# A bias table built beside another attention, and an S5 matrix read from its rows by distance

## The chip, the cores and the metric

The kernel runs on one core of one Trainium2 chip. The metric is the device time of the whole program in microseconds, the median of several runs. A core has TensorE (PE in the profile; PEld is its weight load), VectorE (DVE), ScalarE (ACT), GpSimd (POOL) and SyncE (SP). Here SP issues nearly all DMAs, and it issues them in the order of its queue: an issue that must wait for a buffer holds back all that stand behind it. The kernel before takes 1791.37 us in the median of 3 runs (1785.62 to 1793.07).

## The reference, cut to what matters

The model has two layers over 512 latent and 256 context tokens, width 1024. Each layer sends the modulated input through one wide projection (`h @ w_in`) and then through three mixers: (A) an S5 state-space layer with a gate, (B) neighbourhood attention on the latent grid with a learned relative-position bias, (C) latent attention with compressed keys and values. The branches are gated, projected, added, and projected once more, with a residual and a layer norm.

The change touches two tables that depend on parameters alone, not on tokens:

```python
# (B) the bias: a table looked up by row and column distance, plus a column mask
bias  = rpb[:, idx_r, idx_c].reshape(H, rows, GRID_W, n_lat)
s_lat = einsum('brqhd,brkhd->bhrqk', qr, kg) * NA_SCALE + bias
s_lat = where(mask, s_lat, NEG_INF)
# (A) the scan over time, s_t = a * s_(t-1) + B u_t,  y_t = C s_t, both directions
```

The kernel works (A) out in chunks of 8 tokens. Within a chunk the outputs are the inputs times a block-Toeplitz matrix: its 16 x 16 blocks depend only on the distance j - j', of which there are 15.

## The kernel before, in words

Every matmul of weights with activations is done three times with split operands (high x high, low x high, high x low), in `gemm` at line 232. A weight block arrives by DMA in one of 4 buffers `wr` (`wraw`, line 215), is split by ACT (`wh`) and by DVE or POOL (`wl`), and is then used.

A layer goes through five phases, each with its own SBUF pools:

1. `s5a`: the projections for S5, the gates of branches, the compressed columns (`compressed`, line 1051) and the S5 matrices. `s5_build` makes, for each of 4 blocks of 8 groups, the input, output and scan matrices and the table of 15 distances `kds` (line 683 stores it to DRAM as `kd`, named `s_k` in the profile). Layer 0 builds its four blocks here; layer 1 builds its last two here.
2. `na`: four rounds, each with one `s5_block` (the scan of one block) and the neighbourhood attention of two heads. Line 753 loads the matrix of the chunk, `tp`, into one of 2 buffers `s5_w`; line 758 multiplies it with the inputs.
3. `mla`: four rounds of latent attention for two heads. Behind each round stand gate projections (`gate_n`, `gate_s`) whose result lies in one of 2 buffers `g_t` until it has been stored.
4. `mrg`: the three branch projections, the merge gates, the GELU and gate of S5. `mod_step` works on the next layer's modulation, and in layer 0 `SIDE` puts work for layer 1 between the steps: letter by letter, `T` the S5 tables, `B` one S5 build, `N` the attention bias, `G` the GELU. The GELU's pool takes the place of the pools of T and B, so it waits until these are done with.
5. `outp`: the output projection, the residual and the norm.

Two places matter here. First, at the end of each build, eight DMAs from DRAM to DRAM (line 686) write the matrix of the chunk out in full, `td` (`s_t` in the profile), 16 of its 128 rows each; line 753 later reads it in one piece. Secondly, `na_bias_layer` (lines 350 to 364) makes the bias of one layer: for each head (or two) three DMAs fetch shifted rows of the padded table `rpb_d` into a tile (line 361), POOL adds the column mask `na_mk` (line 145 of the helper), and one DMA stores it to `na_zd` (line 363). Layer 0's bias is made in `s5a`; layer 1's at `N` in `mrg`, in tiles `sb` of the build's ring of 4. The rounds of `na` read `na_zd` at line 1162.

The order of instructions on each engine and on SP is not written by hand: a planner goes through the program with its own estimate of times, and on each engine takes the ready instruction that comes first in the program.

Of the kernel before, what the change touches and what calls it, by code (L numbers as in the profile page):

```python
# [77 lines left out]
SB = (6, 4, 6)  # L78
# [3 lines left out]
SE = {'out0': (2, (1,)), 'out1': (2, (1,)), 'mla0': (4, (0,)), 'mla1': (2, (1,)), 's5a1': (1, (0,)), 'mrg0': (1, (0,)), 'na0': (1, (0,)), 'na1': (1, (0,))}  # L82
SE_REST = (3, (0,))

SIDE = ('T....B.B..N...G.........', '................G.......')

GX = ((0, 0, 1, 1), (1, 1, 1, 0))

# [31 lines left out]
def build(tc, a, out):  # L120
    nc = tc.nc
    V, S, P, PE = nc.vector, nc.scalar, nc.gpsimd, nc.tensor
    Q, PQ = nc.sync, nc.gpsimd
# [7 lines left out]
    def T(p, shape, tag, bufs=1, dt=F32):  # L131
        if isinstance(p, dict):
            p = p.get(tag, p[None])
        return p.tile(list(shape), dt, name=tag, tag=tag, bufs=bufs)
# [22 lines left out]
    dr = pool("dr", DRAM)  # L157
# [45 lines left out]
    def split(h, l, f):  # L203

        act(h, f)
        flip[0] += 1
        n, dve = SE0 if where[0] == "s5a0" else SE.get(where[0], SE_REST)
        e = V if flip[0] % n in dve else P
        tt(e, l, f, h.bitcast(F32), ALU.subtract)
# [140 lines left out]
    def na_bias_layer(l, pd, p, tag, bufs, size):  # L350

        mk = T(p, [48, 32], "na_mk")
        Q.dma_start(out=mk, in_=a["k_namask"])
        zd = T(dr, [48, 8, 480], f"na_zd{l}")
        nh = size // 480
        for h in range(0, 8, nh):
            z = T(p, [128, size + size // 5], tag, bufs)[0:48, 0:480 * nh].rearrange("p (r c) -> p r c", c=32)
            for ty in range(3):
                src = bass.AP(tensor=pd.tensor, offset=pd.offset + (l * 8 + h) * 960 + 8 * ty,
                              ap=[[1, 16], [64, 15 * nh], [1, 32]])  # L360
                Q.dma_start(out=z[16 * ty:16 * ty + 16], in_=src)
            tt(P, z, z, mk.unsqueeze(1).to_broadcast([48, 15 * nh, 32]), ALU.add)
            Q.dma_start(out=zd[:, h:h + nh], in_=z.rearrange("p (h r) c -> p h (r c)", h=nh))
        return zd


    def s5_loads(l, wk, q_=Q):
# [193 lines left out]
    def s5_build(l, b, prm, wk, ng, nsb, ni, out_q=Q):  # L561
# [14 lines left out]
        wd = [T(dr, [128, 1024], f"s5_w{l}{b}{d}") for d in range(2)]  # L576
        od = [T(dr, [128, 1152], f"s5_o{l}{b}{d}") for d in range(2)]
        rd = [T(dr, [128, 2, 384], f"s5_r{l}{b}{d}") for d in range(2)]
        td = T(dr, [128, 8, 128], f"s5_t{l}{b}")
        kd = T(dr, [2, 128, 240], f"s5_k{l}{b}")  # L580
        dcol = dcols[:, l, b]
        gs = slice(8 * b, 8 * b + 8)
# [98 lines left out]
                act(w[:, 128 * g0:128 * (g0 + ng)], q[:, 0:128 * ng])  # L681
            out_q.dma_start(out=wd[d], in_=w)
        out_q.dma_start(out=kd.rearrange("x q n -> q x n"), in_=kds.rearrange("p x m i -> p x (m i)"))
        for j in range(8):
            src = bass.AP(tensor=kd.tensor, offset=kd.offset + (7 - j) * 16, ap=[[240, 16], [32 * 240, 8], [1, 128]])
            Q.dma_start(out=td[16 * j:16 * j + 16], in_=src)
        mats[l].append((wd, od, td, rd))


    def s5_block(mats, b, m8, ud, yd, p, need_ctx):  # L690
        NY = 96 if need_ctx else 64
        wd, od, td, rd = mats
        u = T(p, [128, 8, 128], "s5_u", 1)
        uv = ud.rearrange("(g i) j c -> j i g c", i=16)
        for j in range(8):
            Q.dma_start(out=u[16 * j:16 * j + 16], in_=uv[j])
        sd = [T(p, [128, 8, 128], "s5_s0"), T(p, [128, 8, 97], "s5_s1")]
        P.memset(sd[0][:, :, 0], 0.0)
        P.memset(sd[1][:, :, 96], 0.0)
        ot = []  # L700
        for d in range(2):
            k0 = d * 16 + 4 * b
            w = T(p, [128, 8, 128], "s5_w", 2)
            Q.dma_start(out=w.rearrange("p g n -> p (g n)"), in_=wd[d])
            rc = T(p, [128, 2, 4, 96], "s5_rc", 1)
            Q.dma_start(out=rc.rearrange("p z c n -> p z (c n)"), in_=rd[d])
            o = T(p, [128, 1136], "s5_o", 2)
            Q.dma_start(out=o, in_=od[d][:, 16:1152] if d == 0 else od[d][:, 0:1136])
            ot.append([o[:, 144 * g:144 * g + 128] for g in range(8)])

            mg = T(p, [128, 4, 96], "s5_mg", 1)
            act(mg, m8[:, k0:k0 + 4].unsqueeze(2).to_broadcast([128, 4, 96]))
            P.memset(mg[:, :, 0 if d == 0 else 95], 0.0)

            pv = psw().rearrange("p (r x) -> p r x", r=2)[:, :, 0:384].rearrange("p r (e c) -> p r e c", e=4)
            for r in range(2):
                for g in range(8):
                    e = g % 2
                    PE.matmul(pv[64 * e:64 * e + 64, r, g // 2], w[:, g, 64 * r:64 * r + 64],  # L719
                              u[:, g, 32 * d:32 * d + 96], start=True, stop=True)  # L720

            cv, sv = rc[:, 0], rc[:, 1]
            if d == 1:
                cv, sv = cv[:, :, ::-1], sv[:, :, ::-1]
            va = T(p, [128, 2, 4, 96], "s5_va")
            vb = T(p, [128, 2, 4, 96], "s5_vb")
            for r in range(2):
                tt(V, va[:, r], pv[:, r], cv, ALU.mult)
                tt(V, vb[:, r], pv[:, r], sv, ALU.mult)
            vp = T(p, [128, 2, 384], "s5_vp")  # L730
            fl = lambda z: z.rearrange("p e c -> p (e c)")
            tt(V, vp[:, 0], fl(va[:, 0]), fl(vb[:, 1]), ALU.add)
            tt(V, vp[:, 1], fl(va[:, 1]), fl(vb[:, 0]), ALU.subtract)
            for r in range(2):
                x, m_ = vp[:, r], fl(mg)
                if d == 1:
                    x, m_ = x[:, ::-1], m_[:, ::-1]
                V.tensor_tensor_scan(out=x, data0=m_, data1=x, initial=0.0, op0=ALU.mult, op1=ALU.add)
            va = T(p, [128, 2, 4, 96], "s5_va")
            vb = T(p, [128, 2, 4, 96], "s5_vb")  # L740
            vpv = vp.rearrange("p r (e c) -> p r e c", e=4)
            for r in range(2):
                tt(V, va[:, r], vpv[:, r], cv, ALU.mult)
                tt(V, vb[:, r], vpv[:, r], sv, ALU.mult)
            c_ = slice(1, 97) if d == 0 else slice(0, 96)
            for e in range(2):
                q = slice(64 * e, 64 * e + 64)
                tt(V, sd[d][0:64, e::2, c_], va[q, 0], vb[q, 1], ALU.subtract)
                tt(V, sd[d][64:128, e::2, c_], va[q, 1], vb[q, 0], ALU.add)
        if need_ctx:  # L750
            V.tensor_copy(out=sd[0][:, :, 96:128], in_=sd[0][:, :, 0:32])
        tp = T(p, [128, 8, 128], "s5_w", 2)
        Q.dma_start(out=tp, in_=td)
        ys = T(p, [128, 2, 4, 96], "s5_va").rearrange("p a b c -> p (a b) c")
        py = psw()
        for g in range(8):
            o = py[:, 512 * (g // 4) + 96 * (g % 4):][:, 0:NY]
            PE.matmul(o, tp[:, g], u[:, g, 32:32 + NY], start=True, stop=False)  # L758
            PE.matmul(o, ot[0][g], sd[0][:, g, 32:32 + NY], start=False, stop=False)
            PE.matmul(o, ot[1][g], sd[1][:, g, 1:1 + NY], start=False, stop=True)  # L760
        for s in range(2):
            act(ys[:, 4 * s:4 * s + 4, 0:NY],
                py[:, 512 * s:512 * s + 384].rearrange("p (g c) -> p g c", g=4)[:, :, 0:NY])
        yv = yd.rearrange("(g i) j c -> j i g c", i=16)
        for j in range(8):
            Q.dma_start(out=yv[j][:, :, 0:NY], in_=ys[16 * j:16 * j + 16, :, 0:NY])
# [60 lines left out]
    with st:  # L827
# [5 lines left out]
        mats = [[], []]  # L833
# [4 lines left out]
        for l in range(DEPTH):  # L838
# [40 lines left out]
            with phase("s5a", 3, 2, 1, 1) as sa:  # L879
# [141 lines left out]

                def biases(_):
                    pds.append(na_bias_rows(sp))
                    zds.append(na_bias_layer(0, pds[0], sa, "sb", SB[0], 960))

# [236 lines left out]
            with phase("mla", 2, 2, 2, groups=G_MLA) as mp:  # L1264
# [8 lines left out]
                def gate_n(m):  # L1273
                    th = gate(mp, C_GN + 128 * m)
                    Q.dma_start(out=gn_d[m][:, 0:n_tok], in_=th[:, 0:n_tok])
# [34 lines left out]
                for k in range(2):  # L1310
                    f = early((128, n_tok), c_d[k][:, 0:n_tok])
                    split(cqh[:, k, 0:n_tok], cql[:, k, 0:n_tok], f)

                v_t = T(mp, [128, 6, 512], "mla_v")
                for t in range(6):
# [5 lines left out]
                for i in range(4):  # L1321
# [89 lines left out]
                    Q.dma_start(out=a_m[i][:, 0:n_tok], in_=am[:, 0:n_tok])  # L1411
                    if i < 3:
                        gate_n(2 * i + 2)
                        gate_n(2 * i + 3)
                    for _ in range(GX[l][i]):
                        gate_s(len(ga))

# [2 lines left out]
            with phase("mrg", 4, 3, 0, 1, groups=G_MRG) as mg, contextlib.ExitStack() as es:  # L1420
# [34 lines left out]
                def next_build():  # L1455
                    s5_build(l + 1, len(mats[l + 1]), side["prm"], side["b"], 4, SB[1], NI[1])

                def next_bias():
                    zds.append(na_bias_layer(l + 1, pds[0], side["b"], "sb", SB[1], 480))

                def gelu():

                    sides.close()
# [25 lines left out]
                def side_step(m):  # L1489
                    j = SIDE[l][m]  # L1490
                    if j == "G":
                        gelu()
                    elif j in "TBN" and need_ctx:
                        {"T": next_tables, "B": next_build, "N": next_bias}[j]()

                get = branch_w("w_branch_b")
                for m in range(8):
# [169 lines left out]
```

## Time and profile before

| | |
|---|---|
| median of 3 runs | 1791.37 us (1785.62 to 1793.07) |
| the profiled execution | 1788.85 us, its span 1787.1 us |
| PE busy | 1655.7 us, 93% of the span |
| PEld / DVE / ACT / POOL busy | 78% / 69% / 42% / 21% |
| mean granted TensorE clock | 0.973 of full speed |
| DMA | 264.87 MB, the 16 engines busy for 49.4% with the hardware queue |

The span begins with the first and ends with the last instruction; the profiled execution's own time is 1.75 us longer. The phases of layer 0 lie at about 0 to 225 us (`s5a`), 225 to 490 (`na`), 490 to 702 (`mla`), 702 to 962 (`mrg`) and 962 to 1085 (`outp`); those of layer 1 at 1085 to 1205, 1205 to 1420, 1420 to 1580, 1580 to 1705 and 1705 to the end. In a row of the timeline the first number is the start, the second the duration (with x8, of the eight together), and what stands in brackets is the idle time of that engine just before, with what ended it.

### The profile page before, as it was taken

The page shows a single profiled execution, that of the slowest core. Times are in us where ns is not written, and L with a number is a line of the kernel's source. Part 1 is how long each engine was busy: PE and PEld are TensorE (multiplying, and loading weights), DVE is VectorE, ACT ScalarE, POOL GpSimd, SP SyncE. Part 2 cuts the span into 40 slices and gives each one's busy share as a digit, 9 for nine tenths or more (in the row PEclk, how much of TensorE's full clock was granted, in tenths as well). Part 3 has the DMA queues.
Part 4 walks back from the last instruction along what each step waited for, and adds up shares of the span by engine and source line. Part 5 has one row for each costly group of instructions (what it writes and reads, how often), then busy time and mean ns, then how long its engine had stood idle before and what let it go on. Part 6 is the DMA issues. An engine that isn't in the chain of part 4 may idle for free.

```text
span 1787.1 us, 29011 instructions
## 1 busy us (share of the span) xinstructions
PE 1655.7 (93%) x10808; PEld 1387.4 (78%) x10808; DVE 1238.3 (69%) x2722; ACT 746.9 (42%) x1466; POOL 379.7 (21%) x284
## 2 busy tenths in 40 slices
PE   4899699999989999999799988899999999999996
PEld 2687588888878888878688767788888888788865
DVE  4899948877746564989357688838888666762257
ACT  4423344335355565222243345442344555642241
POOL 2000111012221101201403542001111311245382
PEclk9899799999999999999899999999999999999999
DMA  9567785345321122655756726755554422253462
GB/s 307 158 191 222 207 248 153 94 143 141 84 78 56 58 69 97 232 164 170 192 167 219 189 90 192 225 162 164 156 165 120 126 76 65 83 154 106 130 206 71
DMA packets 273076, 264.87 MB, mean 148 GB/s; under 512 B 70440, under 2 KB 227896, under 8 KB 272936
## 3 DMA queue, kind: packets, MB, share of 16 engines
q1 hardware_dynamic: 271736, 259.93, 49.4%
q0 software_dynamic: 1200, 3.10, 0.5%
q8 instruction: 85, 1.39, 0.3%
q14 instruction: 55, 0.45, 0.1%
HBM read 198.64 MB, written 68.53 MB: 149 GB/s over the span
## 4 chain that ended last, share of the span: by engine, by line
PE 59%; DVE 13%; DMA 6%; ACT 3%; issue 2%; POOL 2%; SPq 1%; DVEq 0%; ACTq 0%; POOLq 0%
PE g L232 35%; PE s L197 5%; PE w L1375 4%; PE s L1403 3%; PE g L1608 2%; DVE sb L145 2%; PE w L1174 2%; PE s L1213 2%; PE w L719 1%; DVE wl L145 1%; DVE ln_rs L148 1%; DMA y<-y_d 1%; DMA wr<-in_w_out 1%; POOL macc L145 1%; PE w L758 1%
## 5 line engine op out<-in xcount | busy, mean ns | idle before, releaser
L232 PE MATMUL g<-hh,wh 128*128 128x512 f32 (+1 forms) x1344 | 479.3, 358 | 16.3 <-ACT wh L142 11.9
L232 PE MATMUL g<-hl,wh 128*128 128x512 f32 (+1 forms) x1344 | 477.0, 355 | 2.7 <-POOL hl L145 1.5
L232 PE MATMUL g<-hh,wl 128*128 128x512 f32 (+1 forms) x1344 | 475.9, 355 | 1.1 <-DVE wl L145 1.1
L232 PEld LDWEIGHTS g<-hh,wh 128*128 128x128 f32 x1344 | 256.3, 191 | 55.9 <-ACT wh L142 12.8
L232 PEld LDWEIGHTS g<-hl,wh 128*128 128x128 f32 x1344 | 256.4, 191 | 37.7 <-DVE hl L148 2.5
L232 PEld LDWEIGHTS g<-hh,wl 128*128 128x128 f32 x1344 | 255.9, 190 | 36.9 <-DVE wl L145 2.8
L142 ACT ACTIVATE wh<-wr 128x1024 fp32r<-128x1024 f32 (+1 forms) x150 | 155.2, 1036 | 227.4 <-PE g L232 139.8
L145 DVE TENSOR_TENSOR wl<-wr,wh 128x1024 fp32r<-128x1024 f32 (+1 forms) x118 | 153.6, 1305 | 114.0 <-ACT wh L142 113.3
L232 PE MATMUL g<-al,wh 128*128 128x512 f32 (+1 forms) x336 | 120.4, 359 | 1.8 <-DVE al L145 1.8
L232 PE MATMUL g<-ah,wl 128*128 128x512 f32 (+1 forms) x336 | 118.7, 358 | 1.2 <-POOL wl L145 1.1
L232 PE MATMUL g<-ah,wh 128*128 128x512 f32 (+1 forms) x336 | 119.7, 361 | 0.0
L145 POOL TENSOR_TENSOR wl<-wr,wh 128x1024 fp32r<-128x1024 f32 (+1 forms) x32 | 74.9, 2339 | 201.7 <-ACT wh L142 183.9
L142 ACT ACTIVATE mla_pt<-s 128x384 f32<-128x384 f32 (+1 forms) x128 | 59.4, 475 | 86.5 <-PE s L197 85.9
L1377 DVE TENSOR_REDUCE mla_sm<-w 128x1 f32<-128x768 f32 (+1 forms) x80 | 67.9, 849 | 34.2 <-PE w L1375 33.3
L145 POOL TENSOR_TENSOR macc<-macc,g_t 128x768 f32<-128x768 f32 (+1 forms) x32 | 56.5, 1769 | 146.3 <-DVE g_t L148 146.3
L232 PEld LDWEIGHTS g<-ah,wh 128*128 128x128 f32 x336 | 63.4, 189 | 14.4 <-issue 3.1
L142 ACT ACTIVATE na_p<-w,na_sm 128x512 f32<-128x512 f32 (+1 forms) x80 | 50.8, 643 | 54.6 <-DVE na_sm L152 48.3
L232 PEld LDWEIGHTS g<-al,wh 128*128 128x128 f32 x336 | 63.9, 190 | 12.3 <-DVE al L145 2.5
L232 PEld LDWEIGHTS g<-ah,wl 128*128 128x128 f32 x336 | 63.9, 190 | 11.6 <-POOL wl L145 2.5
L1608 PE MATMUL g<-woh,hh 128*128 128x512 f32 (+1 forms) x168 | 64.9, 386 | 4.3 <-ACT woh L142 4.2
L142 ACT ACTIVATE mla_p<-w,mla_sm 128x768 f32<-128x768 f32 (+1 forms) x80 | 65.0, 813 | 4.7 <-DVE mla_sm L152 4.5
L1608 PE MATMUL g<-woh,hl 128*128 128x512 f32 (+1 forms) x168 | 64.5, 384 | 0.0
(350 smaller groups left out, 3417.5 us busy)
## 6 DMA issues: line engine op xcount, KB each, us to landing
wr<-in_w_in SPq DMA_DIRECT2D x104, 512.0 KB, 4.6
wr<-in_w_mod SPq DMA_DIRECT2D x32, 512.0 KB, 4.6
s_w<-s_w SPq DMA_DIRECT2D x32, 512.0 KB, 4.3
s_o<-s_o SPq DMA_DIRECT2D x16, 568.0 KB, 5.8
wr<-in_w_out SPq DMA_DIRECT2D x16, 512.0 KB, 3.6
s_o<-sb SPq DMA_DIRECT2D x12, 576.0 KB, 4.4
wr<-in_w_in SPq DMA_DIRECT2D x16, 416.0 KB, 4.6
s_rc<-s_r SPq DMA_DIRECT2D x16, 384.0 KB, 3.2
```

The lines of the kernel that those rows point to most:

```text
L142: return S.activation(out=o, in_=i, func=f, **kw)
L145: return e.tensor_tensor(out=o, in0=x, in1=y, op=op)
L148: V.scalar_tensor_tensor(out=o, in0=x, scalar=s, in1=y, op0=op0, op1=op1)
L197: PE.transpose(o, i, ident[:n, :n])
L232: PE.matmul(o, w[:, k], x[:, k, 0:n], start=(k == 0 and i == 0), stop=(k == nk - 1 and i == 2))
L719: PE.matmul(pv[64 * e:64 * e + 64, r, g // 2], w[:, g, 64 * r:64 * r + 64], u[:, g, 32 * d:32 * d + 96], start=True, stop=True)
L1174: PE.matmul(q[:, e, c:c + 256], qs[:, e, cq], k_[:, e, w0:w0 + 256], start=(j == 0), stop=(j == 1))
L1213: PE.matmul(po[64 * e:64 * e + 64, 0:128], v_t[:, t, 64 * e:64 * e + 64], pt[:, e, n], start=(n == 0), stop=(n == len(kt) - 1))
L1375: PE.matmul(q[:, c], x[0:96, cq], y[0:96, c], start=(j == 0), stop=(j == 2))
L1377: V.tensor_reduce(out=sm[:, 3:4], in_=q[:, k0:TOK], axis=AX.X, op=ALU.max)
L1403: PE.matmul(po[64 * e_:64 * e_ + 64, 0:128], v_t[:, t, 128 * i + 64 * e_:128 * i + 64 * e_ + 64], p2[e_][:, n], start=(n == 0), stop=(n == ...
L1608: PE.matmul(o, x[:, k, tok], w[k][:, c], start=(k == 0 and i == 0), stop=(k == 7 and i == 2))
```

## The change

There are two edits.

The bias of layer 1 is made in `mla` of layer 0. `na_bias_layer` becomes a generator that yields after each head (layer 0's call runs it through at once). Its tile now has the tag `g_t`, the ring of 2 that the gates use, and its mask lies in the pool of `mla`. One head comes between the two `gate_n` of a round and two more behind them, in each of the rounds 0 to 2; `N` goes out of `SIDE`.

The matrix `td` goes. The builds keep only `kd`, and each `s5_block` fills `tp` with eight DMAs straight from `kd`, 16 partitions each, with the access pattern that line 686 had.

```diff
-SIDE = ('T....B.B..N...G.........', '................G.......')
+SIDE = ('T....B.B......G.........', '................G.......')
 # na_bias_layer
             Q.dma_start(out=zd[:, h:h + nh], in_=z.rearrange("p (h r) c -> p h (r c)", h=nh))
-        return zd
+            yield
+        zds.append(zd)
 # s5_build
-        td = T(dr, [128, 8, 128], f"s5_t{l}{b}")
...
-        for j in range(8):
-            src = bass.AP(tensor=kd.tensor, offset=kd.offset + (7 - j) * 16, ap=[[240, 16], [32 * 240, 8], [1, 128]])
-            Q.dma_start(out=td[16 * j:16 * j + 16], in_=src)
-        mats[l].append((wd, od, td, rd))
+        mats[l].append((wd, od, kd, rd))
 # s5_block
         tp = T(p, [128, 8, 128], "s5_w", 2)
-        Q.dma_start(out=tp, in_=td)
+        for j in range(8):
+            src = bass.AP(tensor=kd.tensor, offset=kd.offset + (7 - j) * 16, ap=[[240, 16], [32 * 240, 8], [1, 128]])
+            Q.dma_start(out=tp[16 * j:16 * j + 16], in_=src)
 # latent attention
+                bias = na_bias_layer(l + 1, pds[0], mp, "g_t", 2, 640) if need_ctx else iter(())
...
                     if i < 3:
                         gate_n(2 * i + 2)
+                        next(bias, None)
                         gate_n(2 * i + 3)
+                    for _ in range(2 if i < 3 else 9):
+                        next(bias, None)
 # mrg
-                def next_bias():
-                    zds.append(na_bias_layer(l + 1, pds[0], side["b"], "sb", SB[1], 480))
```

## Rows read from the trace of the kernel before

**Rows 1.** The page's first part: busy time, share of the span, instructions.
```profile
PE 1655.7 (93%) x10808; PEld 1387.4 (78%) x10808; DVE 1238.3 (69%) x2722; ACT 746.9 (42%) x1466; POOL 379.7 (21%) x284
```

**Rows 2.** Busy time by stage: length, each engine's busy time (instructions); clock; DMA.
```profile
72.00:225.00 153.00, 129.25 (x837) 110.67 (x838) 142.93 (x311) 49.98 (x107) 10.09 (x6) 0.92 0.67 198
225.00:490.00 265.00, 257.84 (x1965) 227.46 (x1964) 197.78 (x423) 113.53 (x252) 36.69 (x46) 0.99 0.51 144
490.00:702.00 212.00, 204.58 (x1528) 172.10 (x1529) 119.22 (x285) 121.76 (x276) 31.38 (x17) 0.98 0.19 59
702.00:962.00 260.00, 246.90 (x1528) 204.21 (x1528) 179.56 (x442) 76.62 (x121) 53.69 (x30) 0.98 0.65 198
1205.00:1420.00 215.00, 206.80 (x1574) 181.09 (x1576) 174.23 (x348) 88.07 (x179) 30.05 (x38) 0.98 0.50 145
```

**Rows 3.** The same view around the gap in layer 0's merge.
```profile
869.00:879.00 10.00, 0.36 (x4) 0.16 (x2) 0.00 (x0) 1.33 (x2) 4.17 (x4) 0.74 0.68 171
879.00:884.00 5.00, 4.84 (x12) 3.90 (x13) 2.45 (x2) 1.16 (x2) 0.00 (x0) 0.50 1.18 309
```

**Rows 4.** Timeline of PE: a modulation matmul, and the first matmul after the gap.
```profile
859.94 0.64 PE L306 MATMUL m<-wr,mod_sc 128*32 128x256 f32 x8
...
879.16 0.79 PE L232 MATMUL g<-hh,wh 128*128 128x512 f32 x1 [9.80 <-ACT wh L142]
```

**Rows 5.** Timeline of SP's queue, 848 to 882 us.
```profile
849.63 0.40 SPq L215 DMA_DIRECT2D wr<-in_w_in  x1
...
856.68 5.07 SPq L686 DMA_DIRECT2D s_t<-s_k  x8
...
863.56 3.83 SPq L361 DMA_DIRECT2D sb<-rpb_d  x8
...
873.58 0.45 SPq L215 DMA_DIRECT2D wr<-in_w_in  x1
...
881.28 2.31 SPq L1470 DMA_DIRECT2D y<-y_d  x2
```

**Rows 6.** Timeline of SP, ACT and PE at the end of layer 0's projections.
```profile
223.78 0.55 SPq L1091 DMA_DIRECT2D c<-rms_c  x1
224.56 5.89 SPq L686 DMA_DIRECT2D s_t<-s_k  x8
...
227.89 0.58 ACT L142 ACTIVATE rms_c<-s,mla_g 128x384 f32<-128x384 f32 x1 [7.31 <-DMA c<-rms_c]
...
229.31 0.46 PE L1051 MATMUL w<-wh,hh 128*128 128x416 f32 x1 [2.23 <-ACT wh L142]
```

**Rows 7.** The page's DMA issues: count, KB each, median us from issue to landing.
```profile
s_t<-s_k SPq DMA_DIRECT2D x64, 64.0 KB, 2.4
s_w<-s_t SPq DMA_DIRECT2D x8, 512.0 KB, 3.9
sb<-rpb_d SPq DMA_DIRECT2D x24, 30.0 KB, 2.2
na_zd<-sb SPq DMA_DIRECT2D x8, 90.0 KB, 2.7
```

**Rows 8.** Timeline of SP and PE: the chunk's matrix, its issue and its first use.
```profile
319.97 0.33 SPq L753 DMA_DIRECT2D s_w<-s_t  x1
...
324.60 0.36 PE L758 MATMUL w<-s_u,s_w 128*128 128x96 f32 x2
...
350.68 3.70 SPq L766 DMA_DIRECT2D y_d<-s_va  x8
...
1260.20 1.51 SPq L753 DMA_DIRECT2D s_w<-s_t  x1
...
1265.10 0.41 PE L758 MATMUL w<-s_u,s_w 128*128 128x64 f32 x2 [0.55 <-DMA s_w<-s_t]
```

**Rows 9.** Waits of PE over the span: total, times, longest.
```profile
PE w L758 <- DMA s_w<-s_t: 0.6, 1, 0.6
```

**Rows 10.** Instructions of the mask and the padded table: duration ns min/median/max.
```profile
L145 POOL TENSOR_TENSOR sb<-sb,na_mk x12: 1185/1216/2542, 216.6 to 875.2; 48x480 f32<-48x480 f32 x8, 48x960 f32<-48x960 f32 x4
L361 SPq DMA_DIRECT2D sb<-rpb_d x36: 376/442/1295, 210.2 to 873.1; - x36
```

**Rows 11.** Waits at the head of SP's queue: total, times, longest.
```profile
SPq L1275 <- ACT g_t L142: 162.9, 16, 26.9
```

More of the change, by code (lines that the diff above doesn't have):

```diff
@@ L683, in s5_build @@
         out_q.dma_start(out=kd.rearrange("x q n -> q x n"), in_=kds.rearrange("p x m i -> p x (m i)"))
-        for j in range(8):
-            src = bass.AP(tensor=kd.tensor, offset=kd.offset + (7 - j) * 16, ap=[[240, 16], [32 * 240, 8], [1, 128]])
-            Q.dma_start(out=td[16 * j:16 * j + 16], in_=src)
-        mats[l].append((wd, od, td, rd))
+        mats[l].append((wd, od, kd, rd))
     def s5_block(mats, b, m8, ud, yd, p, need_ctx):
         NY = 96 if need_ctx else 64
-        wd, od, td, rd = mats
+        wd, od, kd, rd = mats
         u = T(p, [128, 8, 128], "s5_u", 1)
@@ L1023, in biases @@
                     pds.append(na_bias_rows(sp))
-                    zds.append(na_bias_layer(0, pds[0], sa, "sb", SB[0], 960))
+                    for _ in na_bias_layer(0, pds[0], sa, "sb", SB[0], 960):
+                        pass
                 gq = T(sp, [128, 3], "mla_g")
@@ L1492, in side_step @@
                         gelu()
-                    elif j in "TBN" and need_ctx:
-                        {"T": next_tables, "B": next_build, "N": next_bias}[j]()
+                    elif j in "TB" and need_ctx:
+                        {"T": next_tables, "B": next_build}[j]()
                 get = branch_w("w_branch_b")
```

## The prediction

> **What bounds the kernel now.** I read the page's busy shares first, then the busy time by stage, then the waits of TensorE, and last the timelines of TensorE and of SP's queue where a wait was long. TensorE is busy for 1655.7 of 1787.1 us [rows 1], so a change saves time only where it takes away idle time of TensorE or a stretch at the lower clock; there are 131 us of idle time in all. By stage [rows 2] this leaves 7.2 us in layer 0's neighbourhood attention, 7.4 in its latent attention, 13.1 in its merge, 8.2 in layer 1's neighbourhood attention, and 23.8 in the second half of the first projections. In these last DVE is busy for 142.93 of 153 us, so that only part of the 23.8 is to be had by freeing a queue.
>
> The longest single wait that the change can reach is in the merge. TensorE stands for 9.80 us until 879.16 us [rows 4]; in the 10 us around it DVE does nothing and ACT 1.33 us [rows 3], so no engine is short of time: a load is late. SP's queue shows which [rows 5]. One weight block is asked for at 849.63 us and the next only at 873.58. Between the two stand the eight copies of `td` (5.07 us of SP) and most of the bias's fetches. A `wr` buffer was free long before: the modulation matmuls that empty one are over at 860.58 [rows 4]. The weight waited behind the bias, whose tile waits for its fetch, then for POOL, then for its store. Behind the gap the clock is at its lower level, 0.50 of full speed, for the 5 us to 884 [rows 3]; 5 us at half speed do the work of 2.5.
>
> **The merge: the bias goes out.** It takes 24 fetches, 8 mask additions on POOL and 8 stores out of a stretch in which SP's order holds back a weight. What is late next? The weight asked for at 873.58 us could be asked for when the last of the three modulation buffers falls free, at the latest at 860.6. From its issue to the restart of TensorE it now takes 879.16 - 873.58 = 5.58 us, so it would be ready at 866.2, before TensorE runs dry at 869.36. So the whole gap goes: 9.80 us and the 2.5 us of the lower clock, 12.3 in sum. The next load of interest is that of the GELU's input, at 881.28 [rows 5]; its pool follows upon the build's, whose tiles the bias holds to the end. It can move up with the bias gone by more than the 12.3 us that TensorE moves up, since the `td` copies end at 861.75 and the bias's stores run on for some 15 us behind them. Bounds: no gain if something else holds the weight, 14 us if the GELU's start was binding as well. I take -12.3.
>
> **The projections and builds: `td` goes out.** Each of the eight builds loses eight issues of SP, 5 to 5.9 us together [rows 5, 6], and the wait before them for `kd` to land. Where does TensorE feel it? At 223.78 a store of compressed columns is issued, and the third ACT pass over them stands for 7.31 us until that store frees its tile, at 227.89; the `td` copies are issued at 224.56, right behind it, and share its way [rows 6]. The weight split behind that pass then lets TensorE restart after 2.23 us of idle time at 229.31. A store that lands in the 2.2 to 2.7 us of other small transfers [rows 7] would free the tile at some 226.3, 1.6 us sooner; with SP's queue shorter before it as well the 2.2 us go. Elsewhere in these stages DVE sets the pace and a freer SP gives nothing. Bounds: 0, and 10 us if a third of the idle time of both projection stages (23.8 us in the first alone [rows 2]) came from SP. I take -2.2, the gap that the rows show.
>
> **The latent attention of layer 0: the bias comes in.** SP gets 24 fetches of 0.44 us [rows 10], 8 stores of some 0.3 us and the mask, 13.5 us over 212; POOL gets 8 additions of 1.22 us, 9.8 us beside its 31.4 [rows 2, 10]. DMA is at a share of 0.19 there [rows 2]. All that is cover enough. What is not free is the ring `g_t`: a head's tile is held for 3 x 0.44 + 2.2 (landing) + 1.2 (POOL) + 0.3 + 2.7 (landing of the store) = 7.7 us [rows 7, 10], 62 us for eight, and behind it stands an ACT pass of a gate, and behind that the softmax's exponentials, which feed TensorE. SP's head stands for up to 26.9 us before a gate's store [rows 11], so a fetch behind it can come late, and POOL, which waits for the fetch, then holds the weight splits behind it. For cover: two buffers over 212 us make 424 us of buffer time, against these 62 and the few gates of each round. Bounds: -1 and +62. I take +2, near the lower one, since TensorE idles only 7.4 us there now with the same ring in use [rows 2].
>
> **The two neighbourhood attentions: eight loads for one.** Now one load of 512 KB is issued and lands in 3.9 us in the median [rows 7]. In layer 0's second round it is issued at 319.97, and the first multiplication that needs it starts at 324.60, 4.6 us on; in layer 1's second round at 1260.20 and 1265.10, with 0.55 us of waiting [rows 8]. All eight together wait 0.6 us [rows 9], so the planner sets the first use just behind the landing. Eight issues take between 3.70 us (eight stores of results [rows 8]) and 5.89 us (the `td` copies [rows 6]), and the last lands 2.4 us behind its start [rows 7]: 6 to 8 us, so 1.4 to 3.7 us late if the first use stayed where it is. The planner knows of eight issues, though, and TensorE has projections to put in front. Bounds: 0 and 8 x 3.7 = 30 us. I take +2.5, a third of a microsecond a round, as its guess for the one load was off by less. SP's next issues there are prefetches, and 4 us later is no harm to them.
>
> The Trainium skill, in "DMA: Bandwidth & Descriptors", section "Rules for kernel authors", speaks against this part: many small transfers should be joined to one large one, since under 64 KB most of the cost is overhead. The rows agree in the sum, not for the single one: 64 KB land in 2.4 us and 512 KB in 3.9 [rows 7], so eight are dearer than one. By that rule this part is a loss in each round, which is the second rival below.
>
> **The sum.** 1788.85 (the profiled execution's own time, 1.75 us above its span) - 12.3 - 2.2 + 2 + 2.5 = 1778.9. The profiled execution is 2.5 us below the median of the runs shown, which spread over 7.5 us; the same sum from the median gives 1781.4. I say 1780.
>
> **The rivals.**
>
> 1. The gates starve on `g_t` (slower). Place: ACT's pass of a gate in rounds 0 to 2 of layer 0's latent attention. Price: 7.7 us for each bias tile that ACT stands before. For it: two buffers, and bias and gate in turn. Against it: that buffer time is mostly free, and DMA is nearly idle there. With three exposed tiles it is 1778.9 - 2 + 23 = 1800; from three on the kernel is slower by over 0.5%, with one or two it is no change.
> 2. The eight loads are late in every round. The first use comes early by 1.4 to 3.7 us, 2.7 in the middle: 8 x 2.7 = 22, so 1778.9 - 2.5 + 22 = 1798. For it: the 0.55 us wait in a tight round. Against it: the planner moves the use.
> 3. The gap in the merge changes its place. With the weight early the GELU's chain becomes the last, or the planner's new order opens a wait of like size elsewhere. For it: the GELU's first loads are issued only 2 us behind the restart of TensorE [rows 4, 5], and several stages have idle time of this size [rows 2]. Against it: the pool is free earlier. The gain is then nil and the costs stay: 1788.85 - 2.2 + 4.5 = 1791; with half of the gap 1785.
> 4. SP's relief is worth more: with 8 us back from the projections beyond the 2.2, 1771.
>
> That the change doesn't do what it says I hold for unlikely: both edits take instructions out of the places named.
>
> **How the numbers follow.** Forecast 0.50, rivals in their order 0.10, 0.12, 0.20, 0.08. Half a per cent, 9 us, is about what a measurement of this kernel tells from no change. Below 1782.4 lies about three quarters of the forecast, all of rival 4 and a fifth of rival 3 (0.37 + 0.08 + 0.04): faster 0.50. Slower is two thirds of rivals 1 and 2: 0.14. The rest is the same: 0.36. The likeliest case alone spans 1774 to 1787; the range reaches up to the first two rivals and down to the fourth: 1769 to 1798.
>
> **What would show it.** In the merge: no wait for a weight split of more than 2 us between 840 and 890, no half clock behind it, the GELU's loads some 15 us earlier. In the projections: the pass over compressed columns no longer waits 7 us for its store. In latent attention: idle time of TensorE under 10 us; waits of ACT's gate passes for `na_zd` stores would show rival 1. In neighbourhood attention: waits of line 758 for its matrix of 2.5 us in sum; 20 or more would show rival 2. The prediction is wrong if the gap stays or if another of its size opens.

## The result, and the profile after

The changed kernel was timed beside the kernel before in three groups of runs, each on one chip.

| group | after, median us | before, median us | ratio, 95% interval |
|---|---|---|---|
| first | 1769.9 (4 runs) | 1788.5 (4) | 0.9896, 0.9867 to 0.9925 |
| second (a0_after) | 1769.2 (4) | 1787.75 (23) | 0.9897, 0.9875 to 0.9920 |
| third (a1_after) | 1771.0 (6) | 1787.6 (17) | 0.9911, 0.9892 to 0.9930 |

So the change saves 16.6 to 18.6 us, 0.9 to 1.0%. The terms of the forecast came to 10 us, and the 1780 us that it gave are 8.5 us less than before took in the first group; the measured 1769.9 us lie 0.9 us above the lower end of its range. The first profiled execution took 1767.77 us, its span 1766.0. Its page begins with this line, to be set against [rows 1]:

```profile
PE 1649.9 (93%) x10808; PEld 1384.7 (78%) x10808; DVE 1237.4 (70%) x2722; ACT 747.3 (42%) x1466; POOL 389.7 (22%) x284
```

TensorE's busy time is only 5.8 us less for the same number of matmuls; 2.65 us of that lie in the merge, where matmuls had run at the lower clock. The other 15.3 of the 21.1 us of span were idle time. (In the latent attention of the first row below, idle time is 7.4 us, as before.) The busy time by stretch, columns as in [rows 2], shows latent attention of layer 0 and then the 30 us in which the gap used to lie:

```profile
490.00:699.00 209.00, 201.60 (x1498) 169.21 (x1497) 118.68 (x281) 120.15 (x271) 41.88 (x25) 0.98 0.23 66
850.00:860.00 10.00, 10.00 (x67) 7.93 (x66) 5.79 (x10) 2.75 (x4) 3.69 (x2) 1.00 1.03 299
860.00:870.00 10.00, 10.00 (x58) 8.78 (x57) 8.69 (x24) 6.12 (x10) 3.68 (x2) 1.00 0.73 210
870.00:880.00 10.00, 10.00 (x58) 8.77 (x57) 7.92 (x19) 6.28 (x9) 3.68 (x2) 1.00 0.43 137
```

TensorE is full and at its upper clock where it stood idle for 9.80 us and then ran at 0.50 [rows 3, 4]. SP's queue in the same place, against [rows 5]: weight after weight goes out, and the GELU's input is asked for at 853.58 us instead of 881.28.

```profile
846.00 1.04 SPq L215 DMA_DIRECT2D wr<-in_w_in  x2
...
852.39 1.13 SPq L215 DMA_DIRECT2D wr<-in_w_in  x2
853.58 1.93 SPq L1471 DMA_DIRECT2D y<-y_d  x2
...
857.51 3.25 SPq L215 DMA_DIRECT2D wr<-in_w_in  x2
```

To see what is the change and what is one execution, I took three profiles of after (first, a0, a1) and two of before (first, b0), cut at the same matmuls. The forecast's terms stand in the last column.

| stage | before, us | after, us | mean difference | forecast |
|---|---|---|---|---|
| projections, layer 0 | 260.8, 261.8 | 259.0, 259.9, 258.9 | -2.0 | -2.2 |
| neighbourhood attention 0 | 232.4, 230.7 | 230.8, 228.9, 228.8 | -2.0 | +1.25 |
| latent attention 0 | 208.7, 208.2 | 209.5, 208.8, 209.4 | +0.8 | +2 |
| merge 0 | 280.3, 280.9 | 267.2, 269.2, 269.8 | -11.9 | -12.3 |
| output 0 | 122.7, 120.0 | 118.4, 118.1, 118.1 | -3.1 | 0 |
| projections 1 | 104.6, 105.6 | 104.8, 104.2, 104.0 | -0.8 | 0 |
| neighbourhood attention 1 | 198.3, 196.6 | 196.5, 196.4, 195.9 | -1.2 | +1.25 |
| the rest | 379.3, 380.3 | 379.9, 380.4, 379.6 | +0.1 | 0 |
| span | 1787.1, 1784.0 | 1766.0, 1765.7, 1764.5 | -20.1 | -10.0 |

("Merge" runs here from the last group of value matmuls of latent attention to the first matmul of the output projection.)

### The profile page after: what moved, and what is told of

Same layout as the page of the kernel before. It is cut to its first block, busy times and chain, and to the rows that moved or that the text cites. A ratio compares the mean times of both kernels' runs of the same rounds, so it can differ in the third digit from the quotient of the medians.

```text
span 1766.0 us, 29009 instructions
## 1 busy us (share of the span) xinstructions
PE 1649.9 (93%) x10808; PEld 1384.7 (78%) x10808; DVE 1237.4 (70%) x2722; ACT 747.3 (42%) x1466; POOL 389.7 (22%) x284
## 4 chain that ended last, share of the span: by engine, by line
PE 62%; DVE 20%; DMA 8%; ACT 3%; issue 3%; POOL 2%; SPq 2%; DVEq 0%; ACTq 0%; POOLq 0%
PE g L232 38%; DVE sb L145 6%; PE s L197 5%; PE w L1376 4%; PE s L1404 3%; PE s L1213 2%; DVE wl L145 2%; PE w L1174 1%; DMA hh<-in_w_mod 1%; PE g L1609 1%; DVE ln_rs L148 1%; PE w L716 1%; PE w L1051 1%; DMA wr<-in_w_mod 1%; DVE r L145 1%
## 5 line engine op out<-in xcount | busy, mean ns | idle before, releaser
L145 POOL TENSOR_TENSOR macc<-macc,g_t 128x768 f32<-128x768 f32 (+1 forms) x32 | 64.3, 2013 | 169.7 <-DVE g_t L148 160.2
```

What stands on the lines that cost most here:

```text
L145: return e.tensor_tensor(out=o, in0=x, in1=y, op=op)
```

## Experiments: the two edits apart

**e1_bias_only** is the changed kernel with the old way of the chunk matrix put back.

```diff
+        td = T(dr, [128, 8, 128], f"s5_t{l}{b}")
...
+            Q.dma_start(out=td[16 * j:16 * j + 16], in_=src)
...
-            Q.dma_start(out=tp[16 * j:16 * j + 16], in_=src)
+        Q.dma_start(out=tp, in_=td)
```

Expected: 

> Only the first edit: layer 1's bias is made beside layer 0's latent attention; the chunk matrix is still written out as td and read in one piece. Theory S (the merge's gap is the change, the rest of the 18.6 us is td's stores and a little chance): 9.80 us of idle time and the half clock behind it go from layer 0's merge, which gets 12 to 14 us shorter; latent attention gets 0 to 2 us longer; sum -11 to -13 us against before, 1775.5 to 1777.5. Rival T (both edits are needed for the gap, since the eight td copies also stand between the two weight issues at 849.63 and 873.58): the merge gets only 4 to 8 us shorter and a wait of 3 us or more for a weight split stays between 840 and 890; 1781 to 1785. Rival U (the bias edit alone is worth all of it): 1768 to 1772.

Measured: 1774.75 us against 1782.8, ratio 0.9960 (0.9944 to 0.9976). In its profile the merge is 268.9 us, latent attention 209.5, and no wait of TensorE in the merge is above 1.23 us. So the bias edit alone takes the whole gap away, with `td`'s copies still in SP's queue at 856.69 us. Rival T falls, and so does U. Theory S has the place but not the time: by the ratio the edit gave 7.1 us (8.05 in the medians), where the theory had 11 to 13 and the profile's merge promised 11.7. Its profiled span, 1771.7 us, is 13.9 us under the mean of the two profiles of before; but before ran at 1782.8 in this group and some 5 us slower in the others, and no profile of it was taken here, so where those 5 us lie stays open.

**e2_td_only** is the kernel before with the second edit alone. Its edit is the `td` part of the change's diff, nothing else.

Expected: 

> Only the second edit: td goes, eight loads from kd fill the chunk matrix where it is used; layer 1's bias stays in layer 0's merge. Theory S: the projections of layer 0 get 1.5 to 2.5 us shorter, the two neighbourhood attentions 1 to 2 us shorter each, as in the profile of the changed kernel; the gap in the merge stays but shrinks by up to 5 us, since 5.07 us of SP issues go out of it; sum -4 to -9 us against before, 1779.5 to 1784.5. The prediction's own term by itself (projections -2.2, attentions +2.5) would give no change in sum, 1788 to 1789 with the gap unchanged. Rival 2 of the prediction (eight loads late in every round) would give 1795 or more.

Measured: 1772.3 us, ratio 0.9946 (0.9934 to 0.9959), 9.6 us less. The merge is 272.7 us, 7.9 less than before. The timeline of TensorE (columns as in [rows 4]) shows half of the gap left:

```profile
870.65 0.80 PE L232 MATMUL g<-hh,wh 128*128 128x512 f32 x1 [4.61 <-ACT wh L142]
```

SP's timeline shows what it waited for, the weight behind the bias:

```profile
846.67 0.42 SPq L215 DMA_DIRECT2D wr<-in_w_in  x1
...
865.59 1.07 SPq L215 DMA_DIRECT2D wr<-in_w_in  x2
...
875.29 0.82 SPq L1468 DMA_DIRECT2D y<-y_d  x2
```

That weight is asked for at 865.59 instead of 873.58 us [rows 5]. Of these 8.0 us, 5.07 are the time of the eight issues and 0.9 the earlier start of the stage (700.9 against 701.8 us); the rest isn't resolved. The 9.6 us are a little more than Theory S's 4 to 9, and the prediction's own terms (no change in sum) and its second rival (1795 or more) fall. Of the places that the theory named, the gap and layer 1's neighbourhood attention came (195.4 us, 2.1 less than the mean of before); layer 0's projections (260.5) are only 0.7 us shorter, and its neighbourhood attention (232.6) is 1.1 longer. The two edits cut at the same gap, so in the merge their gains overlap (11.7 and 7.9 alone, 11.9 together). The ratios multiply to 0.9906, within the interval of the whole change; the profiles say that this product hides an overlap.

**e3_one_load** asks what eight loads cost against one.

```diff
-        for j in range(8):
...
-            Q.dma_start(out=tp[16 * j:16 * j + 16], in_=src)
+        Q.dma_start(out=tp.rearrange("p g n -> p (g n)"), in_=wd[0])
```

Expected: 

> The changed kernel, but the chunk matrix is filled by one DMA of 512 KB instead of eight of 64 KB, from another table already in DRAM, so that the multiplication within a chunk has the wrong matrix: the right one is left out, the work is the same. Theory S (eight loads cost nothing that one would not, since the planner sets the first use 7 to 9 us behind the first issue): within 2 us of the changed kernel, 1768 to 1772. Rival 2 (each round pays for seven more issues on SP): 5 us or more below it, 1765 or less. Rival V (eight short loads are better than a long one, since they go to the matrix in pieces): 2 us or more above it.

Measured: 1767.0 us, 0.9910 (0.9897 to 0.9924). The changed kernel wasn't timed in this group, whose before was 5 us faster than the others', so the expected times can't be held against it; the ratio can, and the changed kernel has 0.9896 to 0.9911. Within some 2.5 us, the half width of the interval, eight loads cost nothing.

**e4_no_bias1** prices the bias at its new place.

```diff
-                            zd = zds[l]
+                            zd = zds[0]
...
-                bias = na_bias_layer(l + 1, pds[0], mp, "g_t", 2, 640) if need_ctx else iter(())
+                bias = iter(())
```

Expected: 

> The changed kernel without layer 1's bias being made at all (its 24 fetches, 8 mask additions and 8 stores are left out; layer 1 reads layer 0's table). This prices the bias at its new place. Theory S: latent attention of layer 0 hides it, all but 0.8 us; 1768 to 1770, the latent attention 0 to 1 us shorter. The prediction's term of +2 us would give 1768. Rival 1 (ACT's gates starve on the shared ring): 4 us or more shorter, 1766 or less, and the difference lies in rounds 0 to 2 of the latent attention.

Measured: 1768.8 us, 0.9920 (0.9904 to 0.9937). Latent attention without the bias takes 209.6 us in the profile, with it 208.8 to 209.5, and TensorE's idle time in it is 7.4 us either way: 24 fetches, 8 additions and 8 stores are free there.

## Experiments: was it SP's order?

**a0_after** and **b0_before** are the two kernels once more.

Expected of a0_after: 

> The changed kernel once more, timed beside the kernel before on the chip of this group of runs. The two edits alone gave 0.996 and 0.9946 of before, which multiplied are 0.9906; e3 and e4, which are the changed kernel less a part, gave 0.991 and 0.992. Theory A (the edits add up, the first pair of runs overstated the gain a little): 0.990 to 0.992, some 15 to 17 us. Rival (the first pair was right, the edits help each other): 0.987 to 0.9895, 19 us or more.

Measured: 0.9897 (0.9875 to 0.9920), between the two cases; the changed kernel does what the first group showed.

Expected of b0_before: 

> The kernel before once more, for a second profile. Theory S: the wait in the merge for a weight split (9.80 us) and the wait for kpe and the compressed columns in the projections (2.23 us) come again, since they follow from the order of SP's queue, within 0.5 us; the stretch of layer 0's output projection, 122.68 us in the first profile and 118.4 to 120.3 in the five profiles of other kernels, comes out at 118 to 120.5 here too, because its 4 us were chance (a late load of x). Rival: it stays at 122 to 123, so both edits, each by itself, shorten it by some 3 us.

Measured: 1785.78 us in its one run. The gap comes again, as 9.49 us, and so does the wait in the projections, though as 2.89 us where 2.23 within 0.5 were expected. The output projection takes 120.0 us, not 122.7: 2.7 us of the first profile's 4.3 were chance.

```profile
878.17 0.79 PE L232 MATMUL g<-hh,wh 128*128 128x512 f32 x1 [9.49 <-ACT wh L142]
```

**e5_bias_pool_queue** leaves layer 1's bias in the merge and takes it off SP, fetches and stores alike.

```diff
-    def na_bias_layer(l, pd, p, tag, bufs, size):
+    def na_bias_layer(l, pd, p, tag, bufs, size, q_=Q):
...
-                Q.dma_start(out=z[16 * ty:16 * ty + 16], in_=src)
+                q_.dma_start(out=z[16 * ty:16 * ty + 16], in_=src)
...
-                    zds.append(na_bias_layer(l + 1, pds[0], side["b"], "sb", SB[1], 480))
+                    zds.append(na_bias_layer(l + 1, pds[0], side["b"], "sb", SB[1], 480, PQ))
```

Expected: 

> The kernel before with layer 1's bias still in layer 0's merge, at the same letter N, but its 24 fetches and 8 stores are issued from POOL's queue instead of SP's. Nothing else is moved: the same bytes, the same mask additions, the same tiles. Theory S (SP's order held back the weight, not the bytes and not POOL): the 9.80 us wait and the half clock behind it go, the merge gets 10 to 13 us shorter, 0.993 to 0.996 of before. Rival W (the bias's traffic, or its tiles that the build's pool must give free, made the gap): the wait stays at 7 us or more, 0.998 to 1.002. Rival X (the gap goes to POOL, which now issues and waits, and whose weight splits stand behind that): a wait of like size for a split made by POOL, 0.998 to 1.005.

Measured: 1788.85 us, 1.0007 (0.9994 to 1.0020), and a merge of 281.0 us: nothing gained, and Theory S, which was mine, falls as a forecast of the time. The first part of it did happen. TensorE is full where the gap was, and 40 us later it isn't (by stretch, as above):

```profile
870.00:880.00 10.00, 10.00 (x57) 8.73 (x56) 2.89 (x2) 1.93 (x3) 9.14 (x14) 1.00 0.68 204
910.00:920.00 10.00, 6.79 (x52) 4.30 (x44) 6.36 (x16) 5.25 (x7) 2.40 (x2) 1.00 0.87 302
920.00:930.00 10.00, 7.25 (x44) 4.55 (x48) 7.16 (x20) 2.42 (x3) 1.24 (x1) 0.66 0.56 184
940.00:950.00 10.00, 7.72 (x45) 6.63 (x44) 6.62 (x9) 4.97 (x7) 1.27 (x1) 0.96 0.86 288
```

The timeline of SP shows why. The GELU's first load, at 881.28 us before, now goes out at 895.86, behind a fourth gate store:

```profile
894.19 0.33 SPq L1517 DMA_DIRECT2D ga_d<-g_t  x1
895.19 0.38 SPq L215 DMA_DIRECT2D wr<-in_ssm_w_glu  x1
895.86 0.87 SPq L1470 DMA_DIRECT2D y<-y_d  x2
```

SP's head waited 20.4 us for the four gate passes between 860 and 900. The bias's last stores were issued at 882.63 us on POOL, in 1.03 us for the two, and land in 4.2 us (median), some 888: the pool that the GELU takes could not be free before that, and the place in SP's queue added some 8 us. TensorE then waits for the GELU's products (1.97 and 2.28 us for `ah`) and for a modulation weight (2.67). This is the prediction's third rival, the gap that changes its place, in another kernel than the one it was made for.

**e8_n_early** moves one letter.

```diff
-SIDE = ('T....B.B..N...G.........', '................G.......')
+SIDE = ('T....BNB......G.........', '................G.......')
```

Expected: 

> The kernel before with one letter of SIDE moved: the bias is made in layer 0's merge right behind the first of the two builds, five steps earlier, still from SP's queue and with td's copies where they were. Theory S (any 24 fetches and 8 stores that wait in turn hold SP's order back wherever they stand beside weight loads): a wait for a weight moves to the new place, 5 us or more, and the merge is at most 5 us shorter; 0.997 to 1.001. Rival Y (it was the meeting of the bias with the td copies of the second build in that one place): the gap goes, the merge is 9 to 13 us shorter; 0.993 to 0.996.

Measured: 1785.9 us, 0.9997 (0.9982 to 1.0013); the merge is 285.1 us. The gap moved with the bias and kept its size, as Theory S said of it; the merge did not get shorter at all but 4.5 us longer:

```profile
840.41 0.79 PE L232 MATMUL g<-hh,wh 128*128 128x512 f32 x1 [10.24 <-ACT wh L142]
```

**e9_bias_gt_ring** and **e10_bias_pool_gt** take the bias out of the build's pool, which the GELU waits for, and into the merge's ring of gate buffers; e10 puts it on POOL's queue as well, as e5 did.

```diff
-    zds.append(na_bias_layer(l + 1, pds[0], side["b"], "sb", SB[1], 480))
+    zds.append(na_bias_layer(l + 1, pds[0], mg, "g_t", 4, 640))
```

Expected of e9_bias_gt_ring: 

> The kernel before with layer 1's bias still at the letter N and still on SP's queue, but its tiles come from the merge's own ring of four gate buffers instead of the build's ring, so that the GELU's pool no longer waits for the bias. e5 took SP's queue out of the way and kept the pool, and gained nothing: the wait of 9.8 us went, and the GELU's first load moved from 881.28 to 895.86 us. Theory B (the bias holds two things in the merge, the weight loads by SP's order and the GELU by the pool, and each alone is as long as the other): with the pool freed alone SP still holds the weight, a wait of 5 to 10 us stays, merge 275 to 281 us, 0.996 to 1.001. Rival P (the pool alone was the matter): the merge falls to 268 to 271, 0.992 to 0.995.

Expected of e10_bias_pool_gt: 

> Both at once: layer 1's bias at the letter N, on POOL's queue and in the merge's own ring of gate buffers. Theory B: neither the weight nor the GELU waits for the bias, the GELU's first load comes before 870 us, and the merge falls to 268 to 273 us, close to the changed kernel's 267 to 269; 0.992 to 0.996. Rival X (POOL's own time for 24 fetches and 8 stores, 17 us at 0.5 us each, takes the place of SP's, in its weight splits and the GELU's multiplications): the merge stays at 277 or more, 0.997 to 1.002.

Measured: e9 1786.95 us, 1.0005 (0.9989 to 1.0020); e10 1807.8 us, 1.0116 (1.0099 to 1.0132), 20 us slower. Theory B named e9's time and its merge, but not the reason, a wait for a weight that stays. With the tile out of the build's ring the planner put the bias 60 us earlier, at 785 to 824 us, beside the S5 build; the 9.8 us gap went, the GELU's load came at 871.19, and the merge fell by no more than 3 us, to 277.7, with short waits for the build (this is the longest) and a clock of 0.83 around them:

```profile
809.27 0.43 PE L659 MATMUL s<-sb,s_b 128*32 128x128 f32 x8 [2.16 <-DVE sb L145]
```

The profiled execution of e9 took 1792.9 us, near the longest of its twelve; 7.7 us of it lie in layer 1's projections (112.9 us against a mean of 105.1 before), and one profile can't tell whether they belong to the kernel.

In e10 the same stretch all but stops TensorE; the view by stretch shows POOL and DVE full and TensorE at 2 of 10 us, then the lower clock:

```profile
820.00:830.00 10.00, 2.10 (x16) 0.92 (x14) 9.96 (x22) 3.05 (x6) 9.98 (x10) 0.74 0.63 161
830.00:840.00 10.00, 3.35 (x32) 1.64 (x36) 8.27 (x15) 1.15 (x3) 2.49 (x3) 0.50 0.89 266
840.00:850.00 10.00, 7.41 (x40) 4.56 (x41) 9.08 (x23) 2.40 (x6) 0.00 (x0) 0.56 0.72 222
```

Its merge takes 303.1 us, within Rival X's "277 or more", but the kernel is slower than that rival had it. Of Theory B the GELU's early load came, at 868.26 us, but not the gain. A modulation weight comes 7.00 us late and the build 5.18 us late, and SP's head stands for the build's stores (17.6 us for five of them between 790 and 850). Whether POOL's work on the bias slowed the build, or only the planner's order for it is worse, these runs don't tell.

**e11_td_stores_kept**, with **a1_after** beside it, prices the 64 copies alone: the changed kernel, with the copies still made and read by nobody.

```diff
+        td = T(dr, [128, 8, 128], f"s5_t{l}{b}")
+        for j in range(8):
...
+            Q.dma_start(out=td[16 * j:16 * j + 16], in_=src)
```

Expected of e11_td_stores_kept: 

> The changed kernel with the 64 copies that write td left in the builds, where nobody reads them now. Beside the changed kernel in this group of runs it prices the copies by themselves, apart from the eight loads that replace the one. Theory S (what td's removal is worth beyond the bias edit, 5 us or so between e1 and the changed kernel, is SP's time and the order of SP in the builds): 4 to 6 us slower than the changed kernel, 1773 to 1775, in layer 0's projections and neighbourhood attention. Prediction's term: 2.2 us slower, in the projections alone. Rival L (the eight loads are better than the one, the copies cost nothing): within 1 us of the changed kernel.

Expected of a1_after: 

> The changed kernel once more, on the chip of this group of runs, so that e9 to e11 have it beside them: 0.988 to 0.991 of before, as in the two groups that had it (0.9896 and 0.9897).

Measured: a1 1771.0 us, 0.9911 (0.9892 to 0.9930); e11 1775.9 us, 0.9937 (0.9920 to 0.9953). The copies cost 4.9 us in the medians; the two intervals overlap, so the size is rough. It is Theory S's size, but not quite its place. Of the stages that the theory named, layer 0's projections are no longer for the copies (257.6 against 258.9 us), and its neighbourhood attention is 3.6 us longer (232.4 against 228.8), part of which is the clock (last section). Layer 1's projections, which no theory named, take 108.3 against 104.0. There a weight stands behind the copies in SP's queue:

```profile
1143.95 5.02 SPq L687 DMA_DIRECT2D s_t<-s_k  x8
...
1150.17 1.16 SPq L215 DMA_DIRECT2D wr<-in_w_in  x2
```

On TensorE the wait that follows:

```profile
1152.84 0.49 PE L232 MATMUL g<-hh,wh 128*128 128x512 f32 x1 [2.39 <-ACT wh L142]
```

In a1, on SP, a weight goes out at 1142.51 us, and TensorE has no such wait:

```profile
1142.51 8.07 SPq L215 DMA_DIRECT2D wr<-in_w_in  x4
```

This wait isn't the whole of the 4.2 us. In e1, with the same copies, TensorE waits 2.16 us in the same place, at 1153.72, and the stage takes 105.1 us; before has the copies too, no such wait, and 104.6 and 105.6 us. So about 2 us are shown as the copies' price there, in the order that the planner makes with the bias moved, and the rest of the 4.9 us isn't located.

## Why the prediction was right, and where it was not

**The merge.** Forecast -12.3 us, the three and two profiles say -11.9. The reading that made it holds in its main part: no engine was short of time, and a weight stood in SP's queue behind the bias. But the prediction named the bias's own chain (fetch, POOL, store) as what held SP up, and that is the smaller part. In the 24.0 us between the two weight issues of before [rows 5] SP issues 38 DMAs, among them 21 fetches, 6 stores and 8 copies, and these issues alone take 17.8 us; at the head of its queue it waits 3.7 us, 2.1 of them for POOL's mask additions. So the weight waited mostly for SP's own time, and e2, with eight issues less, has half of the gap.

What the prediction gave as a side condition, that the GELU must be able to move up too, counted as well: e5 freed the weight and gained nothing, because the GELU's first load came 14.6 us later. e9 had that load 10 us earlier and its merge fell by 3. Which of the two weighs more isn't shown, since the planner set the bias at another time in e9 and e10. A bias in the merge left it at 277.7 to 303.1 us, on either queue and in either ring (five variants, before among them, all with their `td` copies); a bias outside it, or none, at 265.8 to 269.8 (seven profiles). e2 lies between, at 272.7 with half of the gap. So of what was tried only leaving the stage took the whole gap away; a bias at its old time, with both the queue and the pool freed, was not run.

**Latent attention.** Forecast +2, measured +0.8 between the profiles and nothing against e4. POOL waits for a fetch for up to 7.9 us (33.1 in six waits), but no ACT pass of a gate waits for a store of the bias. Such waits were the first rival's condition, and it did not come about.

**The eight loads.** The step that failed: +2.5 us for the two neighbourhood attentions, which became 2.0 and 1.2 us shorter. The prediction left the first use near where it was and charged for the lateness. The planner moved it instead, as the prediction had said that it could; two timelines of after show it for layer 0's second round and layer 1's last (against [rows 8]). The loads on SP:

```profile
318.64 5.09 SPq L752 DMA_DIRECT2D s_w<-s_k  x8
...
1340.26 5.45 SPq L752 DMA_DIRECT2D s_w<-s_k  x8
```

and the multiplications that use them, on TensorE:

```profile
327.63 0.36 PE L757 MATMUL w<-s_u,s_w 128*128 128x96 f32 x2
...
1347.57 0.41 PE L757 MATMUL w<-s_u,s_w 128*128 128x64 f32 x2 [1.68 <-DMA s_w<-s_k]
```

In layer 0 the use stands 9.0 us behind the first issue where it stood 4.6, in layer 1 7.3 us where it stood 4.9, with other matmuls in between, and all 64 loads together make TensorE wait once (total, times, longest):

```profile
PE w L757 <- DMA s_w<-s_k: 1.7, 1, 1.7
```

The issues cost what was forecast (5.09 and 5.45 us for eight). The second rival did not come true: one 64 KB load landed in 2.7 us in the median, all 64 made TensorE wait 1.7 us, and e3's single load of 512 KB is no faster as a kernel. It was the one by the Trainium skill's "DMA: Bandwidth & Descriptors", section "Rules for kernel authors" (many small transfers joined to one); here following that rule would have gained nothing.

Is the gain of some 3 us in the two stages the loads' doing? The clock of single executions alone is worth up to 2 us in layer 0's stage (last section). But TensorE's idle time there is 2.4 to 3.0 us in the five profiles of kernels that have eight loads and no bias in the merge (the three of after, e4 and e11), and 3.7 to 4.6 in the other nine, among them e2 (eight loads, the bias in the merge) and e3 (one load, the bias moved). So some 1.4 us are there whatever the clock, and they go with the order that the planner makes for both edits together; neither edit alone gives them. Half a microsecond of them is a single wait for DVE at some 456 to 461 us, 1.71 us in these five and 2.25 in the others. In layer 1's stage idle time shows nothing of the kind.

**The projections.** Forecast -2.2, measured -2.0 in layer 0, but the agreement is partly luck, and the step that explains it is only half right. The 2.23 us wait behind the held ACT pass [rows 6] is gone, and the pass no longer waits for a store. In its place TensorE waits for DVE, which was near its limit in that stage [rows 2]:

```profile
219.07 0.87 PE L197 MATMUL s<-ident,ct 128*128 128x128 f32 x3 [3.16 <-DVE kpe_t L145]
```

With the copies back, in e11, the pass waits 6.38 us for its store again and TensorE 1.30 us behind it, yet its projections are no longer than a1's. Over all the profiles the six without copies have 258.7 to 260.5 us there, the eight with them 257.6 to 262.1, and the means lie 1.0 us apart. So the wait is the copies' doing, as forecast, but the stage gains less than the wait. The fourth rival, that SP's relief is worth more, held in e2, but in the merge (7.9 us) and not in the projections; with the bias moved, the gap that it shortens is gone already.

**The sum.** The forecast for one execution was 10 us, the profiles give 20.1, the timed medians 16.6 to 18.6; the three profiled executions of after were 1.8 to 4.8 us shorter than the medians of their groups. Of the 10 us between forecast and profiles 5.8 are the neighbourhood attentions, 3.1 the output projection and 1.2 latent attention. Of the output projection's, 1.4 are the one long profile of before (122.7 against 120.0, half of which enters the mean); the other 1.8 stay unexplained, and e3 and e4, with the bias out of the merge too, have 119.9 and 120.3 us there.

The direction and the largest term were right for their reason. That the time lay within the range was luck in part: 1769.9 us is below the likeliest case (1774 to 1787), and the range reached that far down only for the fourth rival's 1771, whose 8 us from the projections did not come. One chance does not follow from its sums: 1798 and 1800 us, the second and first rival, are half a per cent slower than the profiled 1788.85 but not than the median of 1791.37, from which the bound for faster, 1782.4, was taken.

## What to carry to other kernels

Look for a load that stands behind many small issues in an in-order queue, add up what the issues themselves take, and ask what else that work holds up: here a pool as well as a weight, and freeing one of the two was worth nothing. Move such work to a stage whose queue and engines are idle; here another queue or buffer in the same busy stage only moved the wait. When loads become more, look at where their consumer will stand before charging for their issue, and profile each kernel twice before reading a difference of under 3 us in a stage.

## What the runs showed of the hardware

The same wait does not always cost the same. In layer 0's neighbourhood attention TensorE waits 1.7 to 2.3 us for DVE at some 456 to 461 us in every profile. The view by stretch for 450 to 465 us gives the granted clock behind it. In the second profile of before it stays up:

```profile
450.00:465.00 15.00, 11.71 (x90) 10.76 (x90) 14.82 (x28) 1.93 (x3) 2.95 (x2) 1.00 0.31 92
```

In e11, where TensorE is idle for less of it, it falls to 0.77 of full speed in the mean, so that nearly half of the stretch ran at the lower level:

```profile
450.00:465.00 15.00, 13.09 (x79) 12.46 (x78) 10.89 (x21) 4.17 (x9) 3.55 (x3) 0.77 0.25 73
```

The first profiles of before and after have 0.89 there, a0 and a1 have 1.00, and the whole stage differs by 1.7 to 2 us with it between executions of one kernel (232.4 and 230.7 of before; 230.8, 228.9 and 228.8 of after).

DMAs issued by POOL took longer to issue than by SP: 0.57 us for a fetch of the bias and 0.53 for a store in e5 (medians), against 0.44 and 0.32 by SP in before. In e5 they also landed later, the fetch in 4.4 us in the median against 2.2 from SP [rows 7], the store in 4.2 against 2.7:

```profile
sb<-rpb_d POOLq DMA_DIRECT2D x24, 30.0 KB, 4.4
na_zd<-sb POOLq DMA_DIRECT2D x8, 90.0 KB, 4.2
```

That they landed later is not shown to be POOL's doing: in e10, from POOL as well, the medians are 2.8 and 2.3 us, and in e9, from SP, 3.3 and 2.0. The Trainium skill's "DMA: Bandwidth & Descriptors", section "SWDGE vs HWDGE vs iDMA", says that for GpSimd a core's software makes the descriptors and that the hardware path has the faster setup; the issue times agree, and the landings don't decide it.
